# Bonus products earlier and in place, R and y in one copy each, and another spread of the dense work around the chunk steps

## The chip, the cores and the metric

The kernel runs on one core of one Trainium2 chip. The metric is the device time of one execution in microseconds (us). Three runs of the kernel before gave 1312.18, 1314.16 and 1314.32 us; their median is 1314.16 us. The profile shows one more execution, of 1312.45 us, whose instructions span 1310.1 us.

## The reference, cut to what matters

The program is a decoder trunk of two layers over 256 tokens of width 1024. Each layer is a half-step of a gated feed-forward network, a mixing stage, cross attention over 256 memory tokens, and a second half-step. The change lies in the mixing stage alone, which projects the normed input once and feeds two groups of heads, an RWKV-7 recurrence and block-sparse attention ("MoBA"):

```python
x += W_out @ concat[ RWKV-7 time-mix group(P_rwkv), MoBA block-sparse attention group(P_moba) ]

def step(state, inp):
    r_t, w_t, k_t, v_t, kk_t, b_t = inp
    sa = jnp.einsum('bhij,bhj->bhi', state, -kk_t)
    state = (state * w_t[:, :, None, :] + sa[..., None] * b_t[:, :, None, :]
             + v_t[..., None] * k_t[:, :, None, :])
    return state, jnp.einsum('bhij,bhj->bhi', state, r_t)
...
y = ((y - mean) * lax.rsqrt(var + LNX_EPS)).reshape(B, S, W) * ln_g + ln_b
bonus = jnp.sum(r * k * r_k, axis=-1, keepdims=True) * v
y = y + bonus.reshape(B, S, W)
return (y * g).astype(dt)
```

The recurrence has 8 heads of 64. All arithmetic is 32-bit. The kernel multiplies two matrices by splitting each operand into a high part (rounded to TensorE's fast 32-bit form) and a low part (the remainder) and adding three products.

## The kernel before, in words

**Dense work.** Weights come in units of 1 MB by DMA on SyncE's queue into `raw` (two buffers). `unit` splits each into two halves; for each piece `split` makes the high part on ScalarE (`whi`, by `copy`, L83) and the low part on VectorE (`wlo`, a subtraction, L77). There are five buffers each of `whi` and `wlo`, so the splits run a few pieces ahead of TensorE. `mm3` (L99, its matmuls are L97) does the three products. A "column" below is one half of a unit of `w_k`: 24 matmuls of 256 columns.

**The mixing stage** is `mix`, which runs two generators against each other. `rwkv` is the recurrence, in small dependent steps; each of its yields gives a weight `w`. `fill` is dense or independent work. `mix` adds `w` to an account `due` and calls the fill, whose items carry their own weights, until the account is no longer positive. First the fill is four pairs of columns of the attention's q and k (`early`). When `rwkv` yields None, the memory tokens are split into high and low parts (`mem_operand`, which leaves the last subtraction in `marks["memory"]`), and the fill becomes `others`: four items of the memory's values (`v_block(mT, 0)`, which then splits its result into two tiles `v`), the columns k0 to k7 of the memory's keys (`late`), the steps of the block-sparse attention (`att`: scores, turned, values for four pairs of heads) with keys between them, and the first two items of the output projection (`og`), 24 matmuls of 512 columns each. These need all of `att`, and the rest of `og` needs the recurrence's result `yT`: its part for the first 128 tokens (t = 0) needs chunks 0 and 1, the part for t = 1 chunks 2 and 3.

**The recurrence** works on four chunks of 64 tokens. It prepares products of k, r and the decays (`BK`, `rG`, copied into `ZL`), the chunk-wise matrices `XB`, and then inverts triangular matrices of order 64, in 8, 16, 32 and 64: the first part on VectorE in small steps (L729 to L756, each followed by a yield of `2 * XI`; the one at L735 is queued behind `marks["memory"]`), the rest on TensorE by `inverse(cp)`, four levels for each half `cp` of the chunks. `inverse(0)` runs at once, a yield of `XM` = 2.6 behind each level. Level 1 multiplies `UA` by `M` into a PSUM bank, which ScalarE copies to `T1`; level 2 multiplies `T1` with `W2`; levels 3 and 4 complete `W`. `values(c)` transposes v (for two chunks at a time) and copies it into the chunk's `SV` on ScalarE. `inverse(1)`, called `second`, is advanced by one level after each step of the first two chunks.

`chunk(c)` has the steps R (`from_state(0)`, L849, and the copy of the PSUM bank `pz` into `R`), U (`W` times `R`, L859), S (the new state, L867 to L876) and y (L880 to L886). After every second chunk y is normalised (L890 to L900), transposed, multiplied, given the bonus `BV`, and split into `yT` (L913).

`BV` lies in the place of `km`. Its first products `r * r_k * km` (L828, four instructions) are queued behind `marks["inverse"]`, the last transposition of the VectorE part of the inverse; then four pairs of matmuls (L832), a product with v and one with g follow.

**Order and buffers.** The source's order is not the queues' order: a scheduler orders the instructions of each engine by a simulated time and, among those ready, by their place in the source. An instruction traced inside `after(...)` is queued behind the named one on the same engine. Tiles with the tag `e` share 14 buffers; `W`, the two tiles `v`, `ZL`, `XB`, `BT`, `km`, `g`, `G` and the recurrence's r, k and v (all three named `rkv` in the profile) are among them. A tile that finds none free makes its first writer wait for the last reader of another. PSUM has four banks `acc`, two `tr` and two `pm`.

Of the kernel before, what the change touches and what calls it, by code (L numbers as in the profile page):

```python
# [8 lines left out]
FT = mybir.dt.float32  # L9
# [3 lines left out]
OP = mybir.AluOpType  # L13
# [3 lines left out]
S = 256  # L17
# [8 lines left out]
DECAY_C = math.exp(-0.5)  # L26
NEG = -1e30
XA, XBB, XY = 1.3, 0.0, 1.2
XI, XM, XC, XG = 0.8, 2.6, 1.2, 1.0
SQ = 3  # L30
AF_, AO = (7, 5), (3, 3)
HN, HM = 2, ("square", "scaled")
CU = {"b": 1, "ffn": 1, "out": 1, "tail": 2, "a": 2, "q": 2, "qk": 1, "v": 1, "w": 1}
# [7 lines left out]
P_MU, P_W0, P_A0, P_KK, P_KA, P_RK, P_LNG, P_LNB = 40, 54, 58, 62, 66, 70, 74, 78  # L41
# [6 lines left out]
def body(tc, ctx, I, out):  # L48
# [8 lines left out]
    V = nc.vector  # L57
# [3 lines left out]
    marks, hold = {}, []  # L61
# [5 lines left out]
    def H(shape, dt=FT, name="h", tag="e"):  # L67
        return hp.tile(shape, dt, name=nm(name), tag=tag, bufs=HEAP[tag])
# [7 lines left out]
    def tt(out_, a, b, op):  # L76
        return V.tensor_tensor(out=out_, in0=a, in1=b, op=op)  # L77

    def stt(out_, a, s, b, op0, op1):
        V.scalar_tensor_tensor(out_, a, s, b, op0=op0, op1=op1)  # L80

    def copy(out_, in_, **k):
        return A.activation(out_, in_, AF.Copy, **k)  # L83

    def split(hi, lo, src):
        c = copy(hi, src)
        tt(lo, src, hi.bitcast(FT), OP.subtract)
        return c.ins
# [4 lines left out]
    def after(ins):  # L93
        return tc.issue_after(ins[0]) if ins else nullcontext()

    def mm(o, a, b, start=True, stop=True):
        nc.tensor.matmul(o, a, b, start=start, stop=stop, skip_group_check=True)  # L97
# [21 lines left out]

    preload = []  # L120

    def unit(src, cuts, heap=False):
        halves, pieces = preload.pop() if preload else load(src, cuts, heap)
        with ExitStack() as st:
            if hold and hold.pop():
                for m in HM:
                    st.enter_context(tc.issue_after(marks[m]))
            for z in pieces:
                split(*z)
        return halves  # L130

    def rsqrt(v, n, tag):
# [265 lines left out]
    def mem_operand(m):  # L398
        mT = XT()
        for j in range(4):  # L400
            src = m[j // 2][:, 2 * (j % 2):2 * (j % 2) + 2, :]
            copy(mT[j][:, :, 0, :], src)
            marks["memory"] = tt(mT[j][:, :, 1, :], src, mT[j][:, :, 0, :].bitcast(FT), OP.subtract).ins
        return mT

    def xattn(l, xT, kTf, vx, post, following):
# [161 lines left out]
    def half(e):  # L568
        return slice(e * 64, e * 64 + 64)

    def rwkv(l, xT, yT):

        P = lambda c, p: par[:, l, c + p:c + p + 1]
# [30 lines left out]
        for j in range(2):  # L604
            ac = BANK("acc").rearrange("p (c t) -> p c t", c=2)
            for c in range(2):
                p = 2 * j + c
# [53 lines left out]
        for cp in range(2):  # L661
            tt(BK[cp][:, :, :, 0:64], pv(a, cp), pv(Gi, cp), OP.mult)
            tt(BK[cp][:, :, :, 64:128], pv(km, cp), pv(Gi, cp), OP.mult)
        rG = H([128, 4, S], name="rG")
        ZL = [[None, None] for _ in range(2)]
        for cp in range(2):
            Gp = lambda i: G[:, :, 2 * cp:2 * cp + 2, i:i + 64]
            two = lambda z: ch(z)[:, :, 2 * cp:2 * cp + 2, :]
            tt(two(kk), two(kk), Gp(0), OP.mult)
            tt(two(rG), two(r), Gp(1), OP.mult)  # L670
            for e in range(2):
                hs = half(e)
                ZL[e][cp] = H([128, 2, 4, 128], name="ZL")
                copy(ZL[e][cp][hs, :, :, uc(e)], pv(kk, cp)[hs])
                copy(ZL[e][cp][hs, :, :, dc(e)], pv(rG, cp)[hs])
        yield XA
        yield XBB

# [84 lines left out]
        def values(c):  # L763
            if c >= NCH:
                return
            sv = H([128, 4, 2, 2, 64], name="SV", tag="sv")
            t, f = divmod(c, 2)
            if f == 0:
                pvt[:] = [BANK("tr").rearrange("p (c t) -> p c t", c=4)]
                for p in range(4):  # L770
                    nc.tensor.transpose(pvt[0][:, p, :], v[:, p, t * 128:(t + 1) * 128], ident)
            for e in range(2):
                copy(sv[half(1 - e), :, e, :, :],
                     pvt[0][half(f), :, None, e * 64:e * 64 + 64].to_broadcast([64, 4, 2, 64]))
            SV.append(sv)

        values(0)
        values(1)
        for e in range(2):
            nc.gpsimd.memset(SV[0][half(e), :, e, 0, :], 0.0)  # L780
        hq = [slice(e * 64, e * 64 + 32) for e in range(2)]
# [37 lines left out]
                copy(W[hq[e], ix, 32:64], p5[hq[e]])  # L819
            yield XM  # L820

        yield from inverse(0)
        second = inverse(1)

        BV = km
        for p in range(4):
            with after([marks["inverse"]]):
                stt(BV[:, p, :], r[:, p, :], P(P_RK, p), km[:, p, :], OP.mult, OP.mult)  # L828
        for j in range(2):
            pb = BANK("pm").rearrange("p (c t) -> p c t", c=2)  # L830
            for c in range(2):
# [6 lines left out]
        def chunk(c):  # L838
# [4 lines left out]
            def from_state(part):  # L843
                for p in range(4):
                    for e in range(2):
                        o = half(e ^ part)
                        mm(pz[o, p, e, :], ZL[e][cp][:, cc, p, o], sv[:, p, e, 0, :], part == 0 and p == 0, False)

            from_state(0)  # L849
            R = SM([128, 4, 64], name="R", tag="k1")  # L850
            copy(R[half(0)], pz[half(0), :, 0, :])
            V.tensor_copy(R[half(1)], pz[half(1), :, 1, :])
            if c:
                values(c + 1)
            yield XC
# [21 lines left out]
                yield XC  # L877
            for p in range(4):
                for e in range(2):
                    mm(pz[half(1 - e), p, e, :], XB[cp][half(e), cc, p, dc(e)], sv[half(e), p, e, 1, :],  # L880
                       False, True)
            if cc == 0:
                ys[:] = [SM([128, 2, 4, 64], name="y", tag="k2")]
            y = ys[0]
            copy(y[half(1), cc], pz[half(1), :, 0, :])
            copy(y[half(0), cc], pz[half(0), :, 1, :])  # L886
            if cc == 0:
                return

# [25 lines left out]

        for c in range(NCH):
            for w in chunk(c):
                yield w
                if c < 2:
                    next(second, None)  # L920

    def mix(l, xT, post):
        mv = [H([128, 512], name="mv", tag="mo") for _ in range(2)]
# [7 lines left out]
        def v_block(mT, n):  # L931

            v.append([H([128, 2, 512], FR, "v") for _ in range(2)])
            acc = [BANK(("acc", "pm")[n]) for _ in range(2)]
            for u in range(2):
                for i, w in enumerate(unit(I["w_v"][l, 2 * n + u], CU["vw"[n]])):
                    w = tuple(a.rearrange("p (k n) -> p k n", k=2) for a in w)
                    for t in range(2):
                        for j in range(2):
                            k = 4 * u + 2 * i + j  # L940
                            mm3(acc[t], tok(mT, k, t), tuple(a[:, j, :] for a in w), k == 0, k == KT - 1)
                    yield 2.6
            for t in range(2):
                split(v[n][t][:, 0, :], v[n][t][:, 1, :], acc[t])
# [32 lines left out]
        def others(mT):  # L977
            yield from v_block(mT, 0)
            ks = late(mT)
            yield from islice(ks, 4)  # L980
            for i, w in enumerate(att):
                yield w
                if i % 3 == 1:
                    yield from islice(ks, 1)
            yield from ks
            for _ in islice(og, 2):
                yield 5.2
# [214 lines left out]
```

## Time and profile before

| | |
|---|---|
| median of three runs | 1314.16 us (1312.18 to 1314.32) |
| profiled execution, and its span | 1312.45 us, 1310.1 us |
| TensorE (PE) busy | 1276.6 us, 97% |
| VectorE (DVE) busy | 910.0 us, 69% |
| ScalarE (ACT) busy | 756.7 us, 58% |
| GpSimd (POOL) busy | 51.3 us, 4% |
| granted TensorE clock, mean | 0.993 |
| read from HBM | 219.80 MB, 171 GB/s |

The mixing stage of layer 0 lies at about 225 to 393 us, that of layer 1 at about 868 to 1041 us. In the timelines a row gives the start, the time from the first start to the last end, the engine, the line, the operation, out<-in, and the count; in brackets stands the engine's idle time before it and what ended it. A window's row gives its length, then for each engine its busy time and number of instructions, the granted TensorE clock, the DMA engines' share and rate.

### The profile page before, as it was taken

To read this page: it belongs to the slowest core of one execution; us is meant where nothing else is said; L and a number is where in the kernel's file an instruction comes from. 1 tells how busy PE (TensorE), PEld (TensorE's weight loads), DVE (VectorE), ACT (ScalarE), POOL (GpSimd) and SP (SyncE) were. 2 spreads that over 40 slices of the span, in tenths; PEclk is the share of its full clock that TensorE was granted. 3 is DMA by queue.
4 is the path that set the end of the run, shared out by engine and by line. 5 is a ranking of instruction groups with operands and counts; after the bars stand their busy time and mean duration, and the time that the engine had idled before them with its cause. 6 is when DMAs were issued, how large, how long until landed. Compare 5 with 4: busy or idle time off the path is not lost.

```text
span 1310.1 us, 22248 instructions
## 1 busy us (share of the span) xinstructions
PE 1276.6 (97%) x8838; PEld 1101.1 (84%) x8838; DVE 910.0 (69%) x1697; ACT 756.7 (58%) x1423; POOL 51.3 (4%) x73
## 2 busy tenths in 40 slices
PE   8999999998999999999999999999979999999997
PEld 6888888997789888888888888899867898888886
DVE  6797556877688676675576665667866877766644
ACT  6656437765756565555365554576647555655543
POOL 0081000010000000000000000000000000000000
PEclk9999999998999999999999999999999999999999
DMA  8866653344145435555545556344340345355552
GB/s 280 318 238 248 222 209 129 119 172 138 50 142 192 158 129 193 193 188 202 189 161 189 179 179 246 129 170 146 131 146 34 125 166 177 130 192 194 181 175 95
DMA packets 34423, 224.38 MB, mean 171 GB/s; under 512 B 4328, under 2 KB 4752, under 8 KB 9104
## 3 DMA queue, kind: packets, MB, share of 16 engines
q1 hardware_dynamic: 31344, 212.93, 45.9%
q0 software_dynamic: 2400, 9.45, 2.2%
q8 instruction: 69, 1.13, 0.3%
q10 hardware_dynamic: 576, 0.59, 0.1%
q14 instruction: 34, 0.28, 0.1%
HBM read 219.80 MB, written 4.73 MB: 171 GB/s over the span
## 4 chain that ended last, share of the span: by engine, by line
PE 77%; DVE 10%; ACT 6%; DMA 3%; issue 3%; SPq 0%; ACTq 0%; DVEq 0%
PE acc L97 69%; PE pm L97 5%; DVE wlo L77 3%; ACT whi L83 2%; DMA raw<-in_w_f1i_dram 2%; PE tr L202 1%; PE tr L97 1%; DMA raw<-in_w_k_dram 1%; DMA raw<-in_w_mixa_dram 1%; ACT ZL L83 1%; ACT BT L83 1%; ACT UD L83 1%; ACT SV L83 0%; DMA raw<-in_w_o_dram 0%; ACT lg L521 0%
## 5 line engine op out<-in xcount | busy, mean ns | idle before, releaser
L97 PE MATMUL acc<-xt,whi 128*128 128x512 f32 (+1 forms) x2496 | 685.8, 345 | 0.6 <-ACT whi L83 0.4
L77 DVE TENSOR_TENSOR wlo<-raw,whi 128x1024 fp32r<-128x1024 f32 (+1 forms) x456 | 464.5, 1036 | 265.8 <-ACT whi L83 264.8
L83 ACT ACTIVATE whi<-raw 128x1024 fp32r<-128x1024 f32 (+1 forms) x456 | 403.7, 906 | 341.2 <-PE acc L97 220.2
L97 PE MATMUL acc<-xt,wlo 128*128 128x256 f32 x1888 | 532.6, 283 | 0.6 <-DVE wlo L77 0.5
L97 PEld LDWEIGHTS acc<-xt,whi 128*128 128x128 f32 x2496 | 435.0, 191 | 64.8 <-issue 3.4
L97 PEld LDWEIGHTS acc<-xt,wlo 128*128 128x128 f32 x1888 | 360.0, 191 | 3.0 <-DVE wlo L77 2.0
L97 PE MATMUL acc<-whi,hT 128*128 128x512 f32 x704 | 220.7, 393 | 0.0
L97 PEld LDWEIGHTS acc<-whi,hT 128*128 128x128 f32 x704 | 132.3, 188 | 30.1
L97 PE MATMUL acc<-wlo,hT 128*128 128x512 f32 x352 | 138.5, 393 | 0.0
L97 PEld LDWEIGHTS acc<-wlo,hT 128*128 128x128 f32 x352 | 66.2, 188 | 14.7
L77 DVE TENSOR_TENSOR z<-acc,z 128x256 f32<-128x256 f32 x160 | 66.9, 418 | 2.1 <-ACT z L83 2.1
L97 PE MATMUL acc<-wb,xt 128*128 128x512 f32 x240 | 62.0, 400 | 0.0
L83 ACT ACTIVATE z<-acc 128x256 f32<-128x256 f32 x160 | 58.5, 366 | 2.9 <-PE acc L97 2.9
L83 ACT ACTIVATE xt<-tr,par 128x128 fp32r<-128x128 f32 x112 | 38.5, 366 | 28.5 <-PE tr L202 15.5
L97 PEld LDWEIGHTS acc<-wb,xt 128*128 128x128 f32 x240 | 43.3, 188 | 9.6 <-ACT xt L83 0.7
L177 ACT ACTIVATE junk<-x 128x512 f32<-128x512 f32 x36 | 22.7, 632 | 40.2 <-DVE x L80 26.1
L83 ACT ACTIVATE hT<-z 128x256 fp32r<-128x256 f32 x80 | 32.4, 405 | 18.9 <-DVE z L77 18.9
L80 DVE SCALAR_TENSOR_TENSOR xt<-tr,par,xt 128x128 fp32r<-128x128 f32 x112 | 36.2, 346 | 8.2 <-ACT xt L83 8.0
L77 DVE TENSOR_TENSOR z<-z,z 128x256 f32<-128x256 f32 x80 | 36.5, 456 | 7.3
L97 PE MATMUL acc<-whi,oT 128*128 128x512 f32 x128 | 40.5, 394 | 0.4 <-ACT whi L83 0.4
L77 DVE TENSOR_TENSOR hT<-z,hT 128x256 fp32r<-128x256 f32 x80 | 35.5, 443 | 3.2 <-ACT hT L83 3.2
L358 ACT ACTIVATE z<-z 128x256 f32<-128x256 f32 x80 | 32.7, 409 | 4.3 <-DVE z L77 4.3
(260 smaller groups left out, 1210.9 us busy)
## 6 DMA issues: line engine op xcount, KB each, us to landing
raw<-in_w_f2i_dram SPq DMA_DIRECT2D x44, 1024.0 KB, 4.8
raw<-in_w_f1i_dram SPq DMA_DIRECT2D x42, 1024.0 KB, 4.8
raw<-in_w_f1o_dram SPq DMA_DIRECT2D x22, 1024.0 KB, 4.8
raw<-in_w_mixa_dram SPq DMA_DIRECT2D x22, 1024.0 KB, 4.8
raw<-in_w_f2o_dram SPq DMA_DIRECT2D x22, 1024.0 KB, 4.8
raw<-in_w_v_dram SPq DMA_DIRECT2D x8, 1024.0 KB, 4.8
raw<-in_w_k_dram SPq DMA_DIRECT2D x8, 1024.0 KB, 5.0
raw<-in_w_mixo_dram SPq DMA_DIRECT2D x8, 1024.0 KB, 4.8
```

What stands on the lines that cost most here:

```text
L77: return V.tensor_tensor(out=out_, in0=a, in1=b, op=op)
L80: V.scalar_tensor_tensor(out_, a, s, b, op0=op0, op1=op1)
L83: return A.activation(out_, in_, AF.Copy, **k)
L97: nc.tensor.matmul(o, a, b, start=start, stop=stop, skip_group_check=True)
L177: marks["square"] = A.activation(junk, xt[:, n * 512:(n + 1) * 512], AF.Square, scale=1.0 / 32.0, accum_out=ss[:, n:n + 1]).ins
L202: nc.tensor.transpose(p[:, k, :], xs[:, k * 128:(k + 1) * 128], ident)
L358: A.activation(sums[0], sums[0], AF.Silu)
```

## The change

It does six things:

1. The four bonus products move from behind the first inverse to in front of `ZL`, in place over `km`, without the queueing behind `marks["inverse"]`. r times the decay is then written over r, and the tile `rG` is gone.
2. `pz` holds its two parts side by side in the same columns for both halves of the partitions, so that R is one copy of 128 partitions on VectorE (before: one of 64 on ScalarE and one on VectorE), and y one of 128 on ScalarE (before: two of 64).
3. `values(1)` moves behind the first level of `inverse(0)`.
4. `XI` goes from 0.8 to 1.0, five instead of four keys' columns go in front of `att`, and then one behind every fourth step of `att` instead of every third.
5. In the first two chunks the weight of every step is doubled, and the second inverse is advanced before the fill is called, not after it.
6. The second half of the pieces of the first `w_v` unit queues its subtractions behind the first low part of the memory (`marks["first"]`).

```diff
-XI, XM, XC, XG = 0.8, 2.6, 1.2, 1.0
+XI, XM, XC, XG = 1.0, 2.6, 1.2, 1.0
...
-    def unit(src, cuts, heap=False):
+    def unit(src, cuts, heap=False, behind=()):
...
-            for z in pieces:
-                split(*z)
+            for i, z in enumerate(pieces):
+                with after(behind if 2 * i >= len(pieces) else []):
+                    split(*z)
...
-            marks["memory"] = tt(mT[j][:, :, 1, :], src, mT[j][:, :, 0, :].bitcast(FT), OP.subtract).ins
+            marks["memory" if j else "first"] = tt(mT[j][:, :, 1, :], src, mT[j][:, :, 0, :].bitcast(FT), OP.subtract).ins
...
-        rG = H([128, 4, S], name="rG")
+        BV = km
+        for p in range(4):
+            stt(BV[:, p, :], r[:, p, :], P(P_RK, p), km[:, p, :], OP.mult, OP.mult)
...
-            tt(two(rG), two(r), Gp(1), OP.mult)
+            tt(two(r), two(r), Gp(1), OP.mult)
...
-                copy(ZL[e][cp][hs, :, :, dc(e)], pv(rG, cp)[hs])
+                copy(ZL[e][cp][hs, :, :, dc(e)], pv(r, cp)[hs])
...
         values(0)
-        values(1)
...
-        yield from inverse(0)
+        levels = inverse(0)
+        yield next(levels)
+        values(1)
+        yield from levels
         second = inverse(1)
-        BV = km
-        for p in range(4):
-            with after([marks["inverse"]]):
-                stt(BV[:, p, :], r[:, p, :], P(P_RK, p), km[:, p, :], OP.mult, OP.mult)
...
-                        mm(pz[o, p, e, :], ZL[e][cp][:, cc, p, o], sv[:, p, e, 0, :], part == 0 and p == 0, False)
+                        mm(pz[o, p, part, :], ZL[e][cp][:, cc, p, o], sv[:, p, e, 0, :], part == 0 and p == 0,
+                           False)
...
-            copy(R[half(0)], pz[half(0), :, 0, :])
-            V.tensor_copy(R[half(1)], pz[half(1), :, 1, :])
+            V.tensor_copy(R, pz[:, :, 0, :])
...
-                    mm(pz[half(1 - e), p, e, :], XB[cp][half(e), cc, p, dc(e)], sv[half(e), p, e, 1, :],
+                    mm(pz[half(1 - e), p, 1, :], XB[cp][half(e), cc, p, dc(e)], sv[half(e), p, e, 1, :],
...
-            copy(y[half(1), cc], pz[half(1), :, 0, :])
-            copy(y[half(0), cc], pz[half(0), :, 1, :])
+            copy(y[:, cc], pz[:, :, 1, :])
...
             for w in chunk(c):
-                yield w
                 if c < 2:
                     next(second, None)
+                    w *= 2
+                yield w
...
-                for i, w in enumerate(unit(I["w_v"][l, 2 * n + u], CU["vw"[n]])):
+                for i, w in enumerate(unit(I["w_v"][l, 2 * n + u], CU["vw"[n]],
+                                          behind=() if n or u else [marks["first"]])):
...
-            yield from islice(ks, 4)
+            yield from islice(ks, 5)
             for i, w in enumerate(att):
                 yield w
-                if i % 3 == 1:
+                if i % 4 == 1:
                     yield from islice(ks, 1)
```

## The prediction

> **What bounds the kernel now.** I read the page's busy times first, then the idle gaps of PE, then the windows in which they lie.
>
> ```profile
> span 1310.1 us, 22248 instructions
> ...
> PE 1276.6 (97%) x8838; PEld 1101.1 (84%) x8838; DVE 910.0 (69%) x1697; ACT 756.7 (58%) x1423; POOL 51.3 (4%) x73
> ```
>
> PE is the bound: it is idle for 1310.1 - 1276.6 = 33.5 us in all. The change removes no matmul, so it can gain only from idle PE time and from time at a reduced clock. Both are in plain sight in the mixing stage. The next rows are of PE's timeline, layer 0 first.
>
> ```profile
> 302.97 0.74 PE L97 MATMUL tr<-M,UA 32*32 32x32 f32 x64 [1.65 <-DVE M L756]
> ...
> 311.23 0.34 PE L97 MATMUL tr<-T,W 32*32 32x32 f32 x10 [2.95 <-ACT T L83]
> ...
> 316.85 0.69 PE L97 MATMUL tr<-M,XB 32*32 32x32 f32 x32
> 317.48 0.50 PE L97 MATMUL acc<-xt,whi 128*128 128x256 f32 x2
> ...
> 320.53 0.69 PE L97 MATMUL tr<-W,TB 32*32 32x32 f32 x32
> ...
> 331.85 0.66 PE L97 MATMUL tr<-T,W 32*32 32x32 f32 x29 [0.15 <-ACT T L83]
> ...
> 333.04 0.43 PE L97 MATMUL acc<-mpT,mv 128*64 128x128 f32 x3
> ...
> 932.63 0.50 PE L97 MATMUL acc<-whi,xt 128*128 128x512 f32 x1 [1.56 <-DVE xt L77]
> ...
> 948.10 0.28 PE L97 MATMUL tr<-M,UA 32*32 32x32 f32 x11 [1.46 <-DVE M L756]
> ...
> 956.37 0.31 PE L97 MATMUL tr<-T,W 32*32 32x32 f32 x8 [4.45 <-ACT T L83]
> ...
> 983.22 0.18 PE L97 MATMUL tr<-M,XB 32*32 32x32 f32 x1 [2.71 <-issue]
> ```
>
> Four of the six gaps, those at 302.97, 311.23, 948.10 and 956.37, lie in the first inverse: level 1 waits for VectorE's M, level 2 for ScalarE's copy T. The windows put the whole of it in numbers: first the two inverses from the end of column k0, then the chunk steps up to the output projection. The fence behind them shows the clock around two gaps.
>
> ```profile
> 300.89:321.23 20.34, 15.74 (x302) 14.83 (x300) 12.34 (x20) 9.25 (x14) 0.00 (x0) 0.83 0.42 144
> 946.21:966.37 20.16, 14.25 (x302) 13.39 (x300) 12.15 (x19) 9.25 (x14) 0.00 (x0) 0.92 0.42 141
> 321.23:369.40 48.17, 45.56 (x749) 37.58 (x749) 36.87 (x115) 34.48 (x92) 4.87 (x8) 1.00 0.29 97
> 966.37:1018.18 51.81, 47.22 (x749) 39.11 (x749) 36.51 (x115) 34.56 (x92) 2.48 (x4) 0.97 0.20 70
> ```
> ```profile
> 304.70:308.11 3.41, 3.41 (x18) 3.32 (x16) 3.41 (x7) 1.31 (x2) 0.00 (x0) 0.50 0.78 279
> ...
> 946.40:949.80 3.40, 1.95 (x75) 1.69 (x74) 3.37 (x7) 1.06 (x1) 0.00 (x0) 1.00 0.32 133
> 949.80:953.20 3.40, 2.12 (x18) 1.91 (x16) 3.40 (x7) 1.26 (x2) 0.00 (x0) 1.00 0.76 270
> ...
> 301.30:304.70 3.40, 1.75 (x73) 1.72 (x73) 3.37 (x7) 1.06 (x1) 0.00 (x0) 1.00 0.32 130
> ```
>
> A gap costs more than itself. After the window 301.30 to 304.70, in which PE was idle for 1.65 us, the granted clock is 0.50 for the next 3.41 us. After 946.40 to 949.80, idle for 1.45 us, it stays 1.00. So a gap of somewhere above 1.5 us costs up to 3.41 x 0.5 = 1.7 us more if PE has work then.
>
> [...]
>
> **The first inverse: T.** Why is T late? Level 1 ends by 303.71, and T is copied at 310.79. ScalarE's queue:
>
> ```profile
> 303.18 1.06 ACT L83 ACTIVATE whi<-raw 128x1024 fp32r<-128x1024 f32 x1 [4.32 <-DMA raw<-in_w_k_dram]
> 306.80 0.60 ACT L83 ACTIVATE v<-acc 128x512 fp32r<-128x512 f32 x1 [2.56 <-DVE km L80]
> ...
> 308.37 2.40 ACT L83 ACTIVATE SV<-tr 64x512 f32<-64x512 f32 x4
> 310.79 0.38 ACT L83 ACTIVATE T<-tr 128x256 f32<-128x256 f32 x1
> ```
> ```profile
> 305.19 1.58 DVE L80 SCALAR_TENSOR_TENSOR km<-rkv,par,km 128x256 f32<-128x256 f32 x4
> ```
>
> T stands behind the copy into `v`, which waits 2.56 us for VectorE's bonus products, and behind four copies into SV. `v` has no data from them: it waits because its buffer is r's, whose last readers the products are. With the products early and rG gone, r is free once ZL is copied, long before, so `v` finds a buffer: minus 2.56. Two of the SV copies (`values(1)`) go behind level 1, so they stand behind T: minus 1.20. Meanwhile PE gets more to do. I walked the account `due` by hand with both sets of weights. Before: k0 in front of level 1, then k1, k2, k3 and the first scores behind levels 1 to 4. After (seven yields of 2.0 instead of 1.6): k0 and k1 in front of level 1, then k2, k3, k4. A column takes 320.53 - 317.48 = 3.05 us at full clock, more than the gap of 1.65 or 1.46 for M, so that gap closes. T then has to be ready when k2 ends, 0.7 + 3.05 us after level 1 starts at about 304.3 (301.3, when v's transposes ended, plus k1), so by 308.0; 310.79 - 2.56 - 1.20 = 307.0. In layer 1 the gap is 1.5 us larger only because the clock stayed up.
>
> What the inverse would take without idling: three columns 9.15; levels 1, 3 and 4 by their rows 0.74, 0.69 and 0.69; level 2, 333.04 - 331.85 = 1.19 (the second inverse's, at full clock); v's transposes 0.6 (row 336.40 below). Sum 13.0 us against 20.34 and 20.16: losses 7.3 and 7.1. A margin of only 1 us for T, and levels 2 to 3 with VectorE between them, let me leave 1.0 us of loss in each: gain 6.3 + 6.1 = 12.4. Bounds: 14.4 (nothing left), and 3.1 where only the gap for M closes.
>
> **Bonus products early.** They cost the same 1.58 us of VectorE, now between BK and ZL, where it is full.
>
> ```profile
> 256.30 2.36 DVE L77 TENSOR_TENSOR wlo<-raw,whi 128x1024 fp32r<-128x1024 f32 x2
> ```
> ```profile
> 255.22 1.29 ACT L83 ACTIVATE ZL<-rG 64x512 f32<-64x512 f32 x2 [1.20 <-DVE rG L77]
> ```
> ```profile
> 257.25 0.45 PE L97 MATMUL pm<-ZL,BK 64*64 64x128 f32 x8
> 257.63 0.39 PE L97 MATMUL acc<-xt,wlo 128*128 128x256 f32 x1
> ```
>
> Here PE takes the low part (256.30 plus half of 2.36 = 257.5) as soon as it exists, at 257.63. In place over km the products cannot precede BK's last read, so r times decay, its copies into ZL and this split all come 1.58 us later. The ZL matmuls then start at 255.22 + 1.29 + 1.58 = 258.1 instead of 257.25, 0.85 us of idle PE; after that all 32 of the group run (8 took 0.38 here), which covers the wait for the split at 259.1. Cost 0.85 us a layer, 1.7 in all; bounds 0 (the scheduler puts other work there) and 2 x 1.58 = 3.2. No DMA moves with these instructions.
>
> **Memory's low part first.** In layer 1 PE waits 1.56 us for the first xt.
>
> ```profile
> 928.48 3.50 DVE L77 TENSOR_TENSOR wlo<-raw,whi 128x1024 fp32r<-128x1024 f32 x3
> ```
>
> One of the three subtractions ahead goes behind it, 3.50 / 3 = 1.17 us. The moved one is needed a quarter of the value block later, after 12 matmuls of 0.23 us (worked out below), 2.8 us, so it has time. Gain 1.1 in layer 1; in layer 0 PE did not wait, so 0. Bounds 0 and 1.6.
>
> **Copies.**
>
> ```profile
> L83 ACT ACTIVATE y<-pm 64x256 f32<-64x256 f32 x16 | 6.0, 378 | 0.6 <-PE pm L97 0.3
> ...
> L83 ACT ACTIVATE R<-pm 64x256 f32<-64x256 f32 x8 | 3.0, 373 | 1.3 <-PE pm L97 1.3
> ```
>
> The 128-partition copies have the same 256 columns, so I take no longer time for them. ScalarE is rid of 8 x 0.373 + 8 x 0.378 = 6 us. PE's fill covers these; I count 0, with a gain of up to 2 us if the chain of chunks sets the end.
>
> **Fill earlier in the chunk steps.** The doubled weights spend the fill sooner. By the account, before, the last turned, k7, the last values and both output items (some 15 us of PE) were left after chunk 3; after, nothing is: the output items come at the U step of chunk 2 and at the end of chunk 3. The chunk stretches idle for 48.17 - 45.56 = 2.6 and 51.81 - 47.22 = 4.6 us, 2.71 of it the "issue" gap. One thing does not improve: W.
>
> ```profile
> 336.40 0.60 PE L771 MATMUL tr<-con,rkv 128*128 128x128 f32 x4
> ```
> ```profile
> 337.12 1.09 POOL L759 MEMSET W<- 32x512 f32 x2 [5.99 <-issue]
> ```
>
> W gets the buffer of v as its second transposes end (337.00), so chunk 0's U step waits for that. One free buffer more goes to BT and `v`, which stand ahead of W in the source; so W stays late, and work runs ahead of it as now. W stands in POOL's queue behind bias loads that the scores issue, but waits for its buffer, not for them; SP's loads keep their order (w_v, w_k, w_mixo) and each waits for a raw buffer, as now. I count 0 for the chunk steps, from -2 to +4 in all.
>
> At the end of the stage the cover is thinner.
>
> ```profile
> 357.71 0.69 PE L97 MATMUL pm<-SV,BT 128*64 128x64 f32 x16
> ...
> 369.40 0.50 PE L97 MATMUL acc<-whi,yh 128*128 128x512 f32 x1
> ...
> 379.10 1.06 PE L907 MATMUL tr<-con,y 128*64 128x128 f32 x8
> ...
> 381.61 0.39 PE L97 MATMUL acc<-whi,yr 128*128 128x512 f32 x1
> ```
> ```profile
> 384.46 0.69 DVE L77 TENSOR_TENSOR yr<-yf,yr 128x512 fp32r<-128x512 f32 x1
> ```
>
> From chunk 2's S step at 357.71 to the last yr at 385.15 the chain takes 27.4 us now, but padded: fill stands before it on PE and weight splits on VectorE. An output item of 24 matmuls takes (381.61 - 369.40 - 1.06) / 2 = 5.6 us. After the change PE has, from that S step on, the second item (5.6), the t = 0 part of the tail (another 24 matmuls, 5.6), six small groups like level 3's 0.63 and the transposes' 1.06 (4.8 together): 16.0 us. Unpadded I estimate the chain at 18: about 7 for S, R, U and y (3.8 of matmuls, copies of 0.4 between them), and of the 15.7 us that follow now (369.40 to 385.15) 4.7 are the tail's eight half-splits at 3.50 / 6, which can go elsewhere. Exposed: 2 us a layer, 4.0 in all; bounds 0 and 2 x (27.4 - 16.0) = 23.
>
> **The sum.** -12.4 + 1.7 - 1.1 + 0 + 0 + 4.0 = -7.8 us. Against the profiled execution, 1312.45 - 7.8 = 1304.6; that execution is 1.7 us below the median of the runs, against which it is 1306.4. I take 1304.5, by the one from which the terms come.
>
> **Rivals.** (1) The tail runs dry and the kernel is slower: the chain from chunk 2's S step keeps its length because VectorE must do the same splits. At 27.4 us the exposure is 23 us, and with two clock drops 3.4 more: -12.4 + 1.7 - 1.1 + 26 = +14, 1327. It decides from the chain length at which it eats the other terms' 11.8 us: 16.0 + 5.9 = 21.9 us. For it: VectorE's queue is in order and 77% busy in the chunk stretch. Against: list scheduling pulls the tail's matmuls and steps forward, and ScalarE has 6 us less.
>
> (2) T stays late: `v` or T waits for another buffer (the second `v` waits for g as before) and only the gap for M closes: -3.1 + 1.7 - 1.1 + 2 = -0.5, some 1313, no change. For it: the buffers are still short. Against: one of 14 is freed outright.
>
> (3) All goes better: no residual in the inverse (-2.0), no tail cost (-4.0), and the issue gap of 2.71 with its clock loss of 1.7 goes: 1304.5 - 10.4 = 1294. For it: layer 0 ran the same matmuls with no such gap.
>
> (4) The denser stretch brings new issue gaps. At 983.22 PE waited for nothing that the profile shows, in the middle of 32 equal matmuls, after the burst of level 2; after the change levels 1 and 2 stand closer together. Two more such gaps with their clock loss cost 2 x (2.7 + 1.7) = 8.8: 1313, no change. [...]
>
> **How the numbers follow.** Chances: the forecast, between 1299 and 1310, 0.56; (3) 0.18; (2) 0.09; (4) 0.08; (1) in full or in half 0.09. A change of 0.2% (2.6 us) is about what the runs can tell from none. Faster than 1311.5: 0.56 + 0.18 and a part of (2) and (4), 0.78. Same: 0.13. Slower: 0.09. The range goes from (3)'s 1294, with 1 us for its being complete seldom, to 1314, which takes in (2) and (4) and leaves out (1).
>
> **What the profile will show.** Right: no wait of ACT's `v` on DVE `km` at all; T within 4 us after level 1; two columns between k0's start and level 1; the gaps for M, T and the first xt of layer 1 gone, and with them the 0.50 clock windows near 305, 312 and 957; eight copies of R, all on DVE, and eight of y. A new PE gap of up to 1 us near 257 for wlo or ZL. Output matmuls (yh) between the steps of chunks 2 and 3, and PE idle for some us before the last yr matmuls, released by DVE yr. Wrong: T still more than 5 us after level 1; a gap above 6 us before the yr matmuls; "issue" gaps in PE; W's memset far later than 20 us after level 4.

## The result, and the profile after

The changed kernel takes 1294.22 us, the median of four runs (1291.22 to 1295.90); the kernel before, run beside it, 1314.24 us (1312.18 to 1318.43). The ratio is 0.984, with a 95% interval of 0.981 to 0.987: 20 us less, where the prediction had 9.7 less and 1295 as its low end. The profiled executions, 1312.45 and 1295.9 us, differ by 16.6 us; the one lies 1.8 us below its median, the other 1.7 above.

The page's head and busy times:

```profile
span 1294.1 us, 22233 instructions
...
PE 1270.4 (98%) x8838; PEld 1093.8 (85%) x8838; DVE 908.7 (70%) x1697; ACT 751.4 (58%) x1407; POOL 58.0 (4%) x73
```

PE is idle for 1294.1 - 1270.4 = 23.7 us instead of 33.5, and busy for 6.2 us less with as many matmuls. The two, 9.8 + 6.2 = 16.0 us, are the whole difference of the spans. The busy time fits the clock: before, four windows of 3.41 us ran at half clock (0.50 granted, near 305, 312, 957 and 984 us), which costs up to 4 x 1.7 = 6.8 us; after, the granted clock is 1.00 from 7.13 to 1290.55 us, and PE's last matmul ends at 1286.88. The windows answer to those of the prediction; each row gives the length, then for each engine the busy time and its instructions, then the clock. After: the first inverse from the end of column k1 to the end of level 4, in both layers, then from there to the last yr matmul. Before, only the second kind, since the inverse's rows (20.34 and 20.16) stand in the prediction:

```profile
304.90:318.90 14.00, 13.02 (x303) 12.13 (x300) 8.80 (x12) 8.47 (x13) 0.00 (x0) 1.00 0.65 229
944.25:956.98 12.73, 12.73 (x303) 12.00 (x300) 7.69 (x9) 8.37 (x13) 0.00 (x0) 1.00 0.66 242
318.90:390.60 71.70, 67.77 (x849) 54.78 (x850) 57.31 (x161) 42.26 (x103) 5.02 (x8) 1.00 0.30 102
956.98:1028.70 71.72, 67.81 (x850) 54.81 (x850) 57.17 (x161) 42.26 (x103) 2.48 (x4) 1.00 0.23 80
```
```profile
321.23:392.70 71.47, 68.78 (x853) 56.43 (x853) 55.54 (x157) 45.88 (x111) 5.02 (x8) 1.00 0.31 104
966.37:1041.50 75.13, 70.44 (x853) 57.96 (x853) 55.16 (x157) 45.91 (x111) 2.48 (x4) 0.98 0.23 78
```

The inverse holds three columns before and after (302 and 303 matmuls): 20.34 becomes 14.00 and 20.16 becomes 12.73, 13.8 us together. The rest of the stage changes by +0.2 us in layer 0 and -3.4 in layer 1. It holds nearly as many matmuls, but not the same ones: one column (24) less, and instead 12 matmuls and 8 transposes of the next stage, which now run in front of the end of this one. The rows shown make 17.0 us; 1.0 of it is lost elsewhere. The timeline of the first inverse and of the gaps that are left in layer 0:

```profile
258.49 0.50 PE L97 MATMUL acc<-xt,whi 128*128 128x256 f32 x2 [0.32 <-ACT whi L83]
...
300.21 0.60 ACT L83 ACTIVATE v<-acc 128x512 fp32r<-128x512 f32 x1
...
305.52 0.74 PE L97 MATMUL tr<-M,UA 32*32 32x32 f32 x64 [0.18 <-DVE M L760]
...
307.37 0.38 ACT L83 ACTIVATE T<-tr 128x256 f32<-128x256 f32 x1
...
309.26 0.66 PE L97 MATMUL tr<-T,W 32*32 32x32 f32 x29
...
310.93 0.59 PE L97 MATMUL tr<-W,T 32*32 32x32 f32 x45 [0.79 <-issue]
...
330.76 0.34 PE L97 MATMUL tr<-M,XB 32*32 32x32 f32 x10 [0.72 <-DVE W L77]
...
340.20 0.30 PE L97 MATMUL pm<-R,W 64*64 64x64 f32 x2 [0.99 <-ACT W L83]
...
354.19 0.88 PE L97 MATMUL acc<-mpT,mv 128*64 128x128 f32 x12 [0.83 <-ACT mpT L83]
...
383.91 0.50 PE L97 MATMUL acc<-whi,yr 128*128 128x512 f32 x1 [0.81 <-ACT yr L83]
```

`v` waits for nothing, T is copied 1.1 us after level 1 ends (306.26) and is there, at 307.75, 1.5 us before level 2 takes it. What is left are gaps below 1 us, the same in layer 1 but for the one of 0.79.

### The profile page after: what moved, and what is told of

Same layout as the page of the kernel before. It is cut to its first block, busy times and chain, and to the rows that moved or that the text cites. A ratio compares the mean times of both kernels' runs of the same rounds, so it can differ in the third digit from the quotient of the medians.

```text
span 1294.1 us, 22233 instructions
## 1 busy us (share of the span) xinstructions
PE 1270.4 (98%) x8838; PEld 1093.8 (85%) x8838; DVE 908.7 (70%) x1697; ACT 751.4 (58%) x1407; POOL 58.0 (4%) x73
## 3 DMA queue, kind: packets, MB, share of 16 engines
q8 instruction: 69, 1.13, 0.3%
## 4 chain that ended last, share of the span: by engine, by line
PE 78%; DVE 10%; ACT 5%; DMA 4%; issue 2%; SPq 0%; ACTq 0%; DVEq 0%
PE acc L97 71%; PE pm L97 4%; DVE wlo L77 3%; DMA raw<-in_w_f1i_dram 2%; ACT whi L83 2%; PE tr L204 1%; PE tr L97 1%; ACT W L83 1%; DMA raw<-in_w_o_dram 0%; DMA raw<-in_w_mixa_dram 0%; DMA raw<-in_w_v_dram 0%; DMA raw<-in_w_q_dram 0%; DVE BK L77 0%; DVE yf L77 0%; DVE lg L521 0%
```

## The experiments

Each was timed in five rounds beside the kernel before. An interval is about 0.2% wide to either side, so two kernels must differ by some 3 to 4 us in their times; smaller things are read from the gaps.

**The changed kernel again.** 

> The changed kernel once more, timed beside its parts. If the time follows from where TensorE idles, it is 0.984 to 0.988 of the time before, and the profile shows about 24 us of idle TensorE time again, no half-clock window before the end, and small gaps at the same places. The theory that the 0.79 us gap inside level 2 of layer 0 ("issue") belongs to the chip's run and not to the program has it move or vanish here; the theory that it belongs to the program (blocks of instructions that are loaded) has it at the same matmul again, about 310.1 us.

1294.45 us against 1314.45, ratio 0.986 (0.983 to 0.988), PE idle for 24.3 us. The gaps of 0.72 to 0.99 us stand at the same places; one half-clock window, far from the change, is new (a granted clock of 0.98 in the first 100 us). The issue gap is at the same matmuls of level 2, but only 0.18 us long.

**Part 1 alone.**

```diff
+        BV = km
+        for p in range(4):
+            stt(BV[:, p, :], r[:, p, :], P(P_RK, p), km[:, p, :], OP.mult, OP.mult)
...
-            tt(two(rG), two(r), Gp(1), OP.mult)
+            tt(two(r), two(r), Gp(1), OP.mult)
...
```

> The kernel before with part 1 alone: the products early and in place, rG gone. Buffer theory (v's copy waited for r's last readers, and T stood behind it): the wait of 2.56 us goes, T comes 2.5 us sooner, so the gaps of 2.95 and 4.45 us shrink to about 0.4 and 1.9, the gaps for M (1.65 and 1.46) stay; with one or two of the half-clock windows gone the time is 5 to 8.5 us shorter, 1305 to 1309. Rival (the other reordering does it; T stands behind four SV copies and a busy ScalarE anyway): gaps of 2.5 and 4 us remain, 1312 to 1314.

1304.17 us, ratio 0.992 (0.989 to 0.994), 10 us less. The runs lie between 1296.1 and 1307.3. The profiled one is the fastest, 8 us below the median, so its trace shows less loss than most executions have. Its timeline, the first inverse and then layer 1:

```profile
296.91 0.60 ACT L83 ACTIVATE v<-acc 128x512 fp32r<-128x512 f32 x1
...
305.60 0.39 ACT L83 ACTIVATE T<-tr 128x256 f32<-128x256 f32 x1
...
306.04 0.66 PE L97 MATMUL tr<-T,W 32*32 32x32 f32 x29 [1.23 <-ACT T L83]
...
969.14 0.18 PE L97 MATMUL tr<-M,XB 32*32 32x32 f32 x1 [2.54 <-issue]
```

The buffer theory holds: the wait of `v` is gone and the gaps for T fall from 2.95 and 4.45 to 1.23 and 1.13. The gaps for M were expected to stay; here they are 0.67 us in layer 0 and none in layer 1. Why is open.

**The fill's part undone, and alone.** Undone, in the changed kernel (the second is its reverse, in the kernel before):

```diff
-XI, XM, XC, XG = 1.0, 2.6, 1.2, 1.0
+XI, XM, XC, XG = 0.8, 2.6, 1.2, 1.0
...
+                yield w
                 if c < 2:
                     next(second, None)
-                    w *= 2
-                yield w
...
-            yield from islice(ks, 5)
+            yield from islice(ks, 4)
...
-                if i % 4 == 1:
+                if i % 3 == 1:
```

> The changed kernel with parts 4 and 5 undone: one column ahead of level 1 as before, no doubled weights, the second inverse advanced after the fill. Gap theory: only the gaps for M come back (1.65 + 1.46 us, and one half-clock window of 1.7 us), T is in time: some 4.8 us slower than the changed kernel, about 1299; the end of the chunk steps costs nothing in either. Rival 1 (the issue gap of 2.71 us and its clock loss went because the fill was spread otherwise): 4.4 us more, 1303. Rival 2 (the spread is most of the gain): 1306 or above.

> The kernel before with parts 4 and 5 alone. Gap theory: a second column closes the gaps for M (3.1 us, one half-clock window of 1.7 us); T is still behind v and four SV copies, at about 310.8 us in layer 0, and the next column now ends near 309.3, so about 1.5 us of the 2.95 and 3 of the 4.45 us stay: 7 to 9 us faster, 1305 to 1307. Rival 1 (the issue gap goes with the spread): 4.4 us more, 1301 to 1303. Rival 2 (the parts only work together, because T sets the end of the inverse): under 2 us, 1312 to 1314.

Undone: 1301.84 us, ratio 0.990 (0.988 to 0.992), 7.4 us more than the changed kernel. Its PE timeline:

```profile
305.01 0.86 PE L97 MATMUL tr<-M,UA 32*32 32x32 f32 x64 [2.42 <-DVE M L760]
...
973.59 0.21 PE L97 MATMUL tr<-M,XB 32*32 32x32 f32 x1 [2.73 <-issue]
```

The gaps for M are back (2.42 and 1.83), and so is the issue gap, as rival 1 said (1303 by it). Alone: 1315.03 us, ratio 1.001 (1.000 to 1.002), nothing gained:

```profile
307.78 0.60 ACT L83 ACTIVATE v<-acc 128x512 fp32r<-128x512 f32 x1 [2.93 <-DVE km L80]
308.95 1.06 ACT L83 ACTIVATE whi<-raw 128x1024 fp32r<-128x1024 f32 x1 [0.57 <-DMA raw<-in_w_k_dram]
309.92 0.58 ACT L83 ACTIVATE kT<-acc 128x512 f32<-128x512 f32 x1
...
312.93 0.38 ACT L83 ACTIVATE T<-tr 128x256 f32<-128x256 f32 x1
...
313.37 0.85 PE L97 MATMUL tr<-T,W 32*32 32x32 f32 x24 [5.22 <-ACT T L83]
```

The gap for M closes, but `v` still waits and T still stands behind it, and now behind a weight split and `kT` too: T's gap grows from 2.95 to 5.22 (7.00 in layer 1). My expectation had it shrink. The issue gap did not occur in this kernel.

**values(1) in front again.**

```diff
         values(0)
+        values(1)
...
-        levels = inverse(0)
-        yield next(levels)
-        values(1)
-        yield from levels
+        yield from inverse(0)
```

> The changed kernel with values(1) back in front of the first level. Cover theory: T comes 0.6 to 1.2 us later, at about 308.4 to 309.0 instead of 307.75 us; the column behind level 1 ends at 309.3, so nothing is lost: 1294 to 1295, no gap of TensorE ahead of level 2 above 0.3 us. Rival (T has no margin): 1.2 us in each layer and perhaps a half-clock window, 1297 to 1300.

1292.45 us, ratio 0.984 (0.982 to 0.987), and no wait for T: this part is worth nothing once `v` does not wait.

**R and y in two copies again, and in one copy alone.** The diff of the change's second part, in reverse in the changed kernel, and as it is in the kernel before.

> The changed kernel with R and y copied in two halves again (part 2 undone). Theory that fill covers these copies: the only gap in question is the 0.99 us in front of the first U step (R, W), which waits for ScalarE's copies into W; ScalarE has then one more copy of 0.37 us in that queue: up to 0.4 us in each layer, 1294.5 to 1295.5. Rival (the chain of chunks sets the end of the stage): 4 R and 4 y copies of 0.37 us on the chain of each layer, up to 3 us a layer, 1297 to 1300.

> The kernel before with part 2 alone, R and y in one copy each. In the changed kernel these copies were worth 7 us, with the fill spent early; here the fill lies in front of the end of the chain. Theory that copies count only where the chain of chunks is exposed: the chain from the S step of chunk 2 to the transposes of the last y is 21.4 us before and is padded by fill, so only the two gaps in front of the first U step (1.35 and 1.04 us) shrink: 0 to 1.5 us less, 1313 to 1314.5. Rival (they count anywhere, since ScalarE is rid of 6 us): 5 us or more, 1309 or less.

The theory that the copies lie under cover fell in both. Undone: 1301.9 us, ratio 0.991 (0.989 to 0.993), 7.5 us more than the changed kernel's 1294.45, and more than the rival had. Alone: 1308.73 us, ratio 0.995 (0.994 to 0.997), 4.9 us less, close to what the rival had. Two copies, the changed kernel with part 2 undone:

```profile
363.23 0.28 PE L97 MATMUL pm<-SV,BT 128*64 128x64 f32 x2
...
370.48 0.68 PE L97 MATMUL pm<-SV,ZL 128*64 128x64 f32 x14
...
371.19 0.38 ACT L83 ACTIVATE R<-pm 64x256 f32<-64x256 f32 x1
371.25 0.69 DVE L77 TENSOR_TENSOR wlo<-raw,whi 128x512 fp32r<-128x512 f32 x1 [1.29 <-ACT whi L83]
371.97 0.43 DVE L854 COPY R<-pm 64x256 f32<-64x256 f32 x1
...
373.13 0.68 PE L97 MATMUL pm<-R,W 64*64 64x64 f32 x14
...
389.65 0.50 PE L97 MATMUL acc<-whi,yr 128*128 128x512 f32 x1 [0.56 <-ACT yr L83]
```

and one, the changed kernel:

```profile
362.93 0.64 PE L97 MATMUL pm<-SV,BT 128*64 128x64 f32 x16
...
368.54 0.42 DVE L854 COPY R<-pm 128x256 f32<-128x256 f32 x1 [0.35 <-PE pm L97]
...
369.32 0.68 PE L97 MATMUL pm<-R,W 64*64 64x64 f32 x16
```

From chunk 2's S step to the first of the last yr matmuls the chain takes 389.65 - 363.23 = 26.4 us with two copies and 383.91 - 362.93 = 21.0 with one. The copies last no longer than the prediction said (R's 0.38 and 0.43 us in two, 0.42 in one); what the chain loses is in the order of the queues. Of the 5.4 us about 1.1 lie at R itself: with two copies its VectorE half stands behind a weight split until 371.97, 0.8 us after the matmuls for it ended, and 14 of the 16 matmuls of U start 2.0 us after them; with one copy all 16 start 0.8 us after them. About 2.2 us come before R, in the S step: the transposes of y stand between its first and its last matmuls, and a weight split and yr stand before the second half of the new state. The rest, 1.9 us, comes later, most of it between U and y.

How the longer chain becomes 7.5 us is not shown. The windows of the two chains, two copies first:

```profile
363.23:389.65 26.42, 24.88 (x190) 18.36 (x186) 19.78 (x46) 9.31 (x20) 1.09 (x2) 1.00 0.42 145
```
```profile
362.93:383.91 20.98, 20.01 (x171) 15.27 (x167) 16.89 (x42) 7.39 (x16) 1.10 (x2) 1.00 0.43 151
```

PE is idle for 1.5 us in the one and 1.0 in the other, since with two copies 24 matmuls of the next stage run in front of the last yr, and with one 12. In the kernel before, too, the profile shows only 2.0 us less idle time for part 2 alone (its profiled execution, 1310.88 us, is the slowest of its six), 1.2 of them in the gaps in front of a U step, 0.61 us in each layer instead of 1.35 and 1.03; where the rest of its 4.9 us lies stays open.

**The doubled weights undone alone.**

```diff
+                yield w
                 if c < 2:
                     next(second, None)
-                    w *= 2
-                yield w
```

> The changed kernel with part 5 undone alone: the steps of the first two chunks have single weights and the second inverse is advanced after the fill. Tail theory: the small gaps of the changed kernel in the chunk stretch (0.72 before level 3 of the second inverse, 0.83 for mpT, 0.8 for the last yr in each layer, 4.7 us together) come from spending the fill sooner, and go: 1290. Fetch theory, which adds to it: with the second inverse's levels closer together again, a block of instructions due inside a weight load stalls TensorE by up to 2.7 us and 1.7 us of clock: 1294 to 1295, and then the packet starts as that load ends. Rival (the doubled weights themselves gain): 1300 or above with no such stall.

1292.83 us, ratio 0.985 (0.982 to 0.987). The gaps for mpT and the last yr are gone, gaps of 1.09 us in the second inverse and 0.62 in chunk 2 are new, the long issue gap does not come: the doubling neither gains nor costs what can be told. So what undoing the fill cost is not part 5's alone; it is part 4's, or comes of the two together.

**The issue gap.** In the kernel before, PE stood still for 2.71 us in the middle of 32 equal matmuls. DMA traffic of that kernel from 973.3 us to just after the stop at 980.51, and of the next 3.8 us:

```profile
## 3 DMA queue, kind: packets, MB, share of 16 engines
q1 hardware_dynamic: 127, 1.02, 34.9%
q0 software_dynamic: 82, 0.27, 16.3%
...
raw<-in_w_mixo_dram SPq DMA_DIRECT2D x1, 1024.0 KB, 6.4
...
q1 hardware_dynamic: 17, 0.02, 2.5%
q8 instruction: 1, 0.02, 1.6%
```

Queue q8, of the kind `instruction`, moves packets of 16 KB, 69 in all, by count one for some 256 of PE's 17,676 instructions (8838 matmuls and as many weight loads). None starts while the 1 MB weight load is in full flow (all but one of its 128 packets run from 977.82 to 981.05); the next starts at 980.82, and PE goes on at 983.22. By count, an estimate, it was due at 977.4: nearby packets start 95 to 195 instructions after a multiple of 256, the two on either side 143 after. Shifting the count tells whether this is the cause. The edit of the second try; the first has 64 in place of 32:

```diff
         for _ in range(8):
             mm(pw[:, 0:128], warm, warm)
+        for _ in range(32):
+            mm(pw[0:32, 0:32], warm[0:32, 0:32], warm[0:32, 0:32])
```

> The kernel before with 64 more tiny matmuls (32 by 32) in the idle time ahead of the first weights, so that every later instruction of TensorE stands 128 places further on; nothing else differs. Fetch theory: the 2.71 us gap at 980.5 us is TensorE waiting for a block of its instructions, whose 16 KB packet was due near instruction 13,455 (977.4 us) but stood behind a 1 MB weight load that ran from 977.8 to 981.05 us, and started at 980.8. With the shift this packet is due about 3 us sooner, ahead of the load, so the gap and the half-clock window behind it go: 4.4 us less, about 1310 if no other block falls behind a load. Rival (the gap belongs to the place in the work, a wait for a semaphore or a buffer): it stays where it is, 2.7 us, 1314.

This kernel, with 64 of them, took 1317.52 us, ratio 1.002 (1.000 to 1.004), with the gap of 2.67 us at the same matmul. PE had 128 matmuls more, not 64, so with their weight loads 256 instructions: a whole block, which leaves every boundary where it was. So it does not decide. It does show that the gap keeps its place when the count is shifted by a whole block.

> The kernel before with 32 more tiny matmuls in the idle time ahead of the first weights. The 64 of the run before this one became 128 matmuls and 128 weight loads, 256 instructions, so every block of 256 began where it had; 32 shift by half a block. Fetch theory: the packet that is due near instruction 13,455 (977.4 us of the kernel before) is due 128 instructions sooner, at about 974.6 us and so ahead of the weight load of 977.8 to 981.05: no gap near 980 to 987 us in level 3 of the second inverse, and no half-clock window behind it, 4.4 us less, 1310. Rival (the gap belongs to that place of the work): 2.7 us there again, 1314.

1309.4 us, ratio 0.996 (0.995 to 0.998), 4.2 us less, and the 32 matmuls run through:

```profile
976.80 0.74 PE L97 MATMUL tr<-W,T 32*32 32x32 f32 x62
...
979.12 0.69 PE L97 MATMUL tr<-M,XB 32*32 32x32 f32 x32
```

The packet came at 974.82, ahead of the load. (A smaller stall, 0.82 us, is new at 337.86 in layer 0.) A shift by a whole block leaves the gap and a shift by half a block removes it: so I take the gap for an instruction fetch, and the trace of the kernel before has its packet start only as the flow of a weight load ends (980.82 and 981.05 us). The same was tried on the changed kernel:

> The changed kernel with the same 32 tiny matmuls. Fetch theory: the gap of 0.2 to 1.15 us inside level 2 of layer 0 ("issue", 309 to 310 us) goes, since its packet, which stood behind the weight load of 305.4 to 308.8 us, is now due before that load; a new one appears only where a block is due inside a load and the next 256 instructions are short: 1292 to 1295. Rival (it belongs to level 2): the gap stays at 310 us.

1294.53 us, ratio 0.985 (0.983 to 0.987): the gap in level 2 of layer 0 is gone, and no new one above 0.5 us has come in the mixing stages; as the gap was below 1 us, the time can't show it.

**rG kept.**

```diff
+        rG = H([128, 4, S], name="rG")
...
-            tt(two(r), two(r), Gp(1), OP.mult)
+            tt(two(rG), two(r), Gp(1), OP.mult)
...
```

> The changed kernel with r times the decay in a tile of its own again (rG), the products still early. It tells the time of r's last reading from the number of buffers. Theory that the last reader counts: r is read for the last time at about 258 us all the same, so v finds its buffer and T comes at 307.4 to 307.8: 1294 to 1296. Rival (the buffer that rG no longer takes counts): v, ZL or W waits for another one; v's copy or W comes some us later, with gaps of 1 us or more before level 2 or the first U step: 1298 to 1305.

1294.72 us, ratio 0.986 (0.984 to 0.988). `v` waits for nothing, and T comes at 306.22. The time of r's last reading counts, not the number of buffers.

**Products and copies together.** Parts 1 and 2 in the kernel before; the edits are those parts of the change.

> The kernel before with parts 1 and 2 together: products early and in place, R and y in one copy each; fill, values and memory as before. Theory that the parts add: 10 us from the products and 5 from the copies, with the fetch stall in layer 1 (2.7 us and 1.7 of clock) still there: 1298 to 1300; the rest of the changed kernel's gain is that stall. Rival 1 (the copies gain only where the fill is spent early): 1304. Rival 2 (these two parts are everything): 1294 with the stall in place.

1300.11 us, ratio 0.989 (0.987 to 0.991). The parts add: 10 and 5 us alone, 14 together, with the issue gap of 2.54 us still there.

**Memory's low part as before.**

```diff
-                                          behind=() if n or u else [marks["first"]])):
+                                          behind=())):
```

> The changed kernel with part 6 undone: no subtraction of the first w_v unit stands behind the memory's first low part. Gap theory: TensorE waits 1.2 to 1.6 us again for the first xt of layer 1, near 931 us, and nothing else changes: 1295.5 to 1296. Rival (that wait had gone for another reason, or the wait is covered): no such gap, 1294.5.

1302.23 us, ratio 0.991 (0.989 to 0.993), 7.8 us more, and neither theory. There is no gap for the first xt of layer 1. Nor is there one in either shifted copy of the kernel before, which have none of the six parts: the 1.56 us are no lasting property of that kernel. T is late instead, in layer 0:

```profile
309.64 1.06 ACT L83 ACTIVATE whi<-raw 128x1024 fp32r<-128x1024 f32 x1 [4.60 <-DMA raw<-in_w_k_dram]
...
311.19 1.19 ACT L83 ACTIVATE SV<-tr 64x512 f32<-64x512 f32 x2
312.29 0.36 ACT L83 ACTIVATE T<-tr 128x256 f32<-128x256 f32 x1
...
312.70 0.66 PE L97 MATMUL tr<-T,W 32*32 32x32 f32 x29 [3.72 <-ACT T L83]
```

The other order of subtractions on VectorE changed the scheduler's order on ScalarE too: a weight split that waits 4.60 us for its DMA now stands ahead of SV and T. In layer 1 the gap for T is 2.64 us; the two gaps and one half-clock window behind the first, 1.7 us, make up the loss.

**Two combinations.** Single weights with the 32 tiny matmuls, and single weights with values(1) in front.

> The changed kernel with part 5 undone (single weights) and the 32 tiny matmuls ahead of the weights. Theory that the doubled weights bring nothing by themselves: gaps of about 1.1 and 0.5 us in each layer as without the shift, and the 0.87 us gap inside level 2 of layer 0 gone, since its packet is due before the load: 1291 to 1293. Rival (a packet falls behind another load): one gap of up to 2.7 us and 1.7 of clock elsewhere, 1295 to 1297.

> The changed kernel with parts 3 and 5 undone: values(1) in front of the first level and single weights. Each alone left the time as it was or 2 us lower. Theory that T has cover and the doubled weights bring nothing: 1291 to 1293. Rival (each alone used the same slack, so that T or the chain of chunks is late with both undone): a gap of 1 us or more in front of level 2, 1296 or more.

1292.74 us, ratio 0.983 (0.981 to 0.985), and 1292.08 us, ratio 0.983 (0.981 to 0.985). Both are faster than the kernel before; from the changed one (0.986 and 0.984) they can't be told apart.

## Why the prediction was right and wrong

The sum had -7.8 us, and the spans differ by 16.0. Of these 8.2 us the inverse explains 1.4. Nearly all the rest lies in the stage behind the inverse, which the sum had at +4.0 and which came out at -3.2.

**Right: the first inverse**, its largest term, -12.4 us. Measured -6.3 and -7.4, 13.8 together. The gaps for M and T went, and so did the half-clock windows. Part 1 alone and rG kept show that r's last reader was the cause. That T came when worked out (307.0 forecast, 307.37 measured, in layer 0) is in part luck: one SV copy, not two, went behind T, and level 1 started at 305.52 instead of 304.3. The residual of 1.0 us a layer was too much: 0.98 of idle PE in layer 0, 0.79 of it the fetch, nothing in layer 1. The credit to `values(1)` (1.20 us) was for nothing.

**Wrong: "R/y copies ... I count 0".** The step that failed is the sentence "PE's fill covers these". Undoing the copies cost 7.5 us, and the chain from chunk 2's S step grew by 5.4 us; alone, with the old fill still in place, they gained 4.9. The step priced the copies by how long they last and missed that they change what stands in which queue. R's half behind a weight split is about 1.1 us of the 5.4; how the whole becomes time stays open.

**Wrong: the tail, +4.0, and the chunk steps, 0.** Measured together +0.2 in layer 0 and -3.4 in layer 1. The chain was 21.0 us even to the first of the last yr matmuls, not 18, so its estimate was too short; but so was that of the cover: PE is busy for 20.0 us of it, not 16.0, above all because the next stage's value block runs ahead into the gap (12 matmuls of 0.23 us in front of the last yr), which I had not counted as PE work. Two errors nearly cancelled; what is left is a gap of 0.81 us a layer instead of 2. Rival (1) fails by the same step: with two copies the chain is 26.4 us, near its 27.4, and PE is still busy for 24.9 of them. The -3.4 of layer 1 is the fetch stall and its clock, 2.71 + 1.7, of which small new gaps take a part back. The prediction left the stall standing in its sum, and only rival (3) let it go; it comes back with the old fill (2.73 us).

**Wrong reason: memory's low part, -1.1.** The gap of 1.56 us is not there without the part either, and not in the shifted copies of the kernel before, so the term stood on one execution. The part is worth 7.8 us by another way, the place of T on ScalarE.

**Products early, +1.7**: a gap of 0.32 us at 258 in each layer, 0.6.

So rival (3), with 0.18, is nearest to what happened: its three parts, no residual, no exposed tail, no issue gap, came for the most part. That it gave the very 1294 is in part luck. It was counted from the profiled execution, 1.7 us below the median, and from the median it would be 1296; and the gain of the copies was in none of its parts. The low end of the range, 1295, which puts 1 us above rival (3) "for its being complete seldom", was the last step that failed. Of rival (4) a part came: issue gaps of 0.79 and 0.18 us in level 2 of layer 0, in the changed kernel's two profiles, with the clock still at 1.00 behind them.

## What to carry to other kernels

When an instruction is late, ask what stands ahead of it in its engine's queue and what that waits for: T was late through `v`, then through a weight split, and never through its own data. Don't price a copy at nothing because other work covers it: two copies made one gained 4.9 us even where the fill was as before. When fill is moved, count as cover also what the next stage can run ahead. An idle time with no releaser in a burst of short matmuls can be an instruction fetch behind a large transfer (2.71 us in the kernel before); compare the instruction queue's packets with the loads before looking for a semaphore.

## What was not expected of the hardware

**Instruction packets came as weight loads ended.** In the stalls of the kernel before and of the changed one the packet started as the flow of a 1 MB load ended, and PE went on 2.4 us after the packet's start: 980.82 against 981.05 us, and PE at 983.22, in the kernel before; 308.54 against 308.78, and PE at 310.93, in the changed one. A load is 128 packets of 8 KB in the profile. In the kernel before the packet started 3.4 us after it was due by count (the estimate of 977.4 above). Why it comes only then is not shown.

**The length of a gap did not tell whether the clock falls.** The prediction put the limit above 1.5 us. Windows of the changed kernel with two copies (part 2 undone):

```profile
979.20:982.60 3.40, 2.41 (x54) 1.66 (x50) 1.15 (x5) 3.26 (x9) 0.01 (x1) 1.00 0.53 159
982.60:986.00 3.40, 3.35 (x36) 2.83 (x37) 1.22 (x5) 2.53 (x8) 0.00 (x0) 0.50 0.38 157
986.00:989.40 3.40, 3.40 (x33) 2.94 (x29) 1.68 (x8) 1.79 (x5) 0.00 (x0) 0.50 0.00 0
```

0.99 us of idle time in a window with 54 matmuls was followed by two windows at half clock. A gap of as much, 0.99 us in front of 978.29, left the clock at 1.00 in the changed kernel. A longer one left it alone too, in layer 1 of the kernel with memory's part undone, where PE was busy for only 0.98 us of 3.40:

```profile
953.52 0.66 PE L97 MATMUL tr<-T,W 32*32 32x32 f32 x29 [2.64 <-ACT T L83]
```
```profile
951.10:954.50 3.40, 0.98 (x86) 0.98 (x89) 1.23 (x1) 3.34 (x7) 0.00 (x0) 1.00 0.65 258
954.50:957.90 3.40, 3.40 (x63) 3.23 (x54) 2.17 (x4) 1.27 (x3) 0.00 (x0) 1.00 0.09 19
```

So there is no limit between 0.99 and 2.64 us that holds in these runs; what else decides is not shown. Nor is it shown why the runs of most kernels with gaps above 1 us (parts 1, 2 and both alone; the fill or memory's part undone) spread over 6 to 11 us and those of the changed one over 4 to 5; those of the fill alone, with gaps of 5 and 7 us, spread over 3.6.
